# Two-tensor elementwise instructions on VectorE alone, in a list-scheduled encoder trunk of four layers

## The chip, the cores and the metric

The kernel runs on one core of a Trainium2 chip. The metric is the device time of one execution in microseconds (us); lower is better. Where several executions are given, the median is compared.

## What is computed

The reference is an encoder trunk of four residual layers over an input of 256 tokens by 1024 channels, in float32. Each layer is a token mixer followed by a SwiGLU feed-forward network (FFN), each behind an RMS norm and with its result added to the residual. The mixer is RWKV-7 time mixing in layers 0 and 3, stick-breaking attention in layer 1, and attention over keys selected by an indexer ("DSA") in layer 2.

```python
D_MODEL = 1024; SEQ = 256; DEPTH = 4; HEAD_DIM = 64; D_FF = 2816

def rms_norm(x, g):
    return x * lax.rsqrt(jnp.mean(x * x, axis=-1, keepdims=True) + RMS_EPS) * g

def swiglu(h, w_gu, w_down):
    g, u = jnp.split(h @ w_gu, 2, axis=-1)
    return (jax.nn.silu(g) * u) @ w_down

# end of rwkv7_time_mix: y is the output of the recurrence
    y = ((y - mu) * lax.rsqrt(var + RW_GN_EPS)).reshape(B, S, D) * ln_w + ln_b
    y = y + (jnp.sum(rh * kh * r_k, axis=-1, keepdims=True) * vh).reshape(B, S, D)
    out = (y * g).astype(h.dtype) @ w_out

# rope, used for the queries and keys of DSA
    return jnp.concatenate([x1 * cos - x2 * sin, x1 * sin + x2 * cos], axis=-1)
```

## The kernel before

**Tiles.** Channels lie on the partitions, tokens along the free dimension. The residual is four tiles `xt` of 128 partitions by 2 x 256 float32. Every weight is streamed from HBM in pieces of 128 x 1024 (`raw`) and split into a high part and the rest of it: `wh`, a cast (ScalarE or VectorE), and `wl = raw - wh`, always on VectorE. Activations are split in the same manner (`xg` for the normed input, `yhl`, `rhl`), and TensorE multiplies high by high, high by low and low by high.

**The order of the work.** Nothing is issued where it is written. Each call on a queue object (`pe`, `dve`, `act`, `pool`, `sp`, or `anye`, the "any" queue) is recorded by `Plan.record` (line 318), with a cost in ns from `_cost` (line 235). An instruction on `anye` is recorded with several engines as alternatives, from the table `ALTS` (line 201); one that reads or writes PSUM loses GpSimd as an alternative. `Plan._schedule` (line 420) then simulates the five engines with those costs: at each step the engine that is free first takes the ready instruction of the highest rank (the longest chain of costs behind it). An instruction with alternatives is skipped by an engine if another one would finish it earlier by the planner's costs (`elsewhere`, line 490); VectorE's cost counts double there (`BIAS = {"vector": 2.0}`). GpSimd's modelled cost of a two-tensor instruction is 2.1 ns per element of the row plus 150. `emit` (line 650) issues the planned list in its order; each engine works through its own part in that order, and the one line 661 issues every instruction of it. So L661 in the profile is not a place in the program, and the names of the tiles tell what an instruction is.

**Warm-up matmuls.** Where the planned TensorE has a gap, or where nothing ready keeps it filled enough, `keep_warm` (line 480) puts in two matmuls (`WARMERS = 2`) into a bank `warm_o` that nobody reads (line 1564).

**The instructions of `anye.tensor_tensor`.** There are five such lines:

```python
anye.tensor_tensor(nstate["acc"], nstate["acc"], sq, op=ALU.add)   # 836: sqa, before an FFN, stick or DSA
anye.tensor_tensor(nstate["acc"], nstate["acc"], sq, op=ALU.add)   # 848: sq, before an RWKV layer
anye.tensor_tensor(sd, sd, pr[:, p], op=ALU.add)                   # 1297: ysd, end of RWKV
anye.tensor_tensor(sd, sd, gT[:, p], op=ALU.mult)                  # 1298: ysd, end of RWKV
anye.tensor_tensor(b, a, cosb, op=ALU.mult)                        # 1435: rope in DSA (qk, sbt)
```

`prep_chunk` (line 826) prepares the input of the next sub-layer, one `xt` tile at a time as soon as the last output product has been added to it: a square on ScalarE (`sq`), its sum over the four tiles (`sqa`, on `anye`), and two `xg` pairs, the high half on ScalarE, the low one on VectorE. The FFN's first matmuls (`gate`, line 887 on) read `xg`; the sum `sqa` goes through TensorE into `rstd`, which is needed when the products are taken out of PSUM. In RWKV, `post` (line 1286) runs once for each of eight head pairs: variance by a matmul (`vb`), logarithm and exponential on ScalarE, a multiply, an affine step, the two `ysd` steps, and the split into `yhl`. Four `post` results make one half of the input of the output product `po` (`out_half`), which then is added to `xt`. In DSA `rope` splits its input (`rhl`) for an exact rotation on TensorE (`qrot` for queries and keys) and multiplies by the cosine on `anye`.

Of the kernel before, what the change touches and what calls it, by code (L numbers as in the profile page):

```python
# [187 lines left out]
class Queue:  # L188
# [5 lines left out]
    def __getattr__(self, method):  # L194
# [4 lines left out]
          AF.Tanh: "sigmoid_and_others", AF.Silu: "silu_and_others"}  # L199

ALTS = {("any", "copy"): [("scalar", "copy"), ("vector", "tensor_copy")],
        ("any", "tensor_tensor"): [("vector", "tensor_tensor"), ("gpsimd", "tensor_tensor")],
        ("any", "memset"): [("gpsimd", "memset"), ("vector", "memset")]}


# [1523 lines left out]
```

## Time and profile before

| | before |
|---|---|
| median of 3 executions | 1474.14 us (1473.09 to 1474.48) |
| the profiled execution | 1473.95 us |
| its span in the profile | 1472.2 us |
| mean granted TensorE clock | 0.999 |
| instructions in the span | 26233 |
| busy: TensorE (PE) | 1447.0 us, 10434 instructions |
| busy: VectorE (DVE) | 1107.1 us, 2026 |
| busy: ScalarE (ACT) | 718.3 us, 1348 |
| busy: GpSimd (POOL) | 61.3 us, 57 |

A row of the grouped instructions reads: line, engine, operation, written tile <- read tiles, shapes and types, count | busy us, mean ns of one | idle time of the engine just before them, and what ended most of it. A row of the timeline reads: start, duration, engine, line, operation, tiles, shape, count, and in brackets the engine's idle time before it with its releaser. A row of the waits reads: who waits <- for whom: total us, times, longest. PEld is TensorE's loading of weights, SP the engine that issues DMAs.

### The profile page before, as it was taken

The numbers are of one execution on the slowest core, as the hardware profiler recorded it, in microseconds if no ns is written. First come the engines' busy times: TensorE is split into PE (matmuls) and PEld (weight loads), VectorE is DVE, ScalarE is ACT, GpSimd is POOL, SyncE is SP. The second block draws the span as 40 slices with busy tenths as digits, with TensorE's granted clock in tenths as the row PEclk, the third lists the DMA queues.
The fourth block names the chain that finished last, engine by engine and source line by source line (L and its number), as shares of the span: only waits on it lengthen the run. The fifth ranks groups of instructions, "written<-read, shape, count | busy, mean of one in ns | idle before, by whom it ended". The sixth has DMA issues, their size and how long they took to land.

```text
span 1472.2 us, 26233 instructions
## 1 busy us (share of the span) xinstructions
PE 1447.0 (98%) x10434; PEld 1228.1 (83%) x10434; DVE 1107.1 (75%) x2026; ACT 718.3 (49%) x1348; POOL 61.3 (4%) x57
## 2 busy tenths in 40 slices
PE   9999999999999999999999989999999999999998
PEld 6788788888888888888977868888877877888887
DVE  7297478998566779986789978986474884789864
ACT  2344665444447655444546755444325256654442
POOL 0000010000000010000100010000100001200000
PEclk9999999999999999999999999999999999999999
DMA  7234135655554445555634445555523430455653
GB/s 254 91 107 144 36 101 172 194 183 194 175 183 136 130 158 186 198 187 181 192 113 130 129 144 172 186 193 183 197 93 108 129 101 18 130 175 182 196 188 132
DMA packets 77803, 224.55 MB, mean 153 GB/s; under 512 B 23536, under 2 KB 23792, under 8 KB 77424
## 3 DMA queue, kind: packets, MB, share of 16 engines
q1 hardware_dynamic: 77680, 222.87, 46.4%
q8 instruction: 82, 1.34, 0.4%
q14 instruction: 41, 0.34, 0.1%
HBM read 219.70 MB, written 3.15 MB: 151 GB/s over the span
## 4 chain that ended last, share of the span: by engine, by line
PE 86%; DVE 9%; ACT 2%; DMA 2%; issue 1%; SPq 0%; POOL 0%; DVEq 0%
PE up L661 17%; PE dn L661 16%; PE gate L661 16%; PE qk L661 5%; PE po L661 4%; PE kp L661 4%; PE rp L661 4%; PE vps L661 3%; PE z L661 2%; DVE wl L661 2%; PE vp L661 2%; PE warm_o L1564 1%; PE Y L661 1%; PE sc L661 1%; DVE xg L661 1%
## 5 line engine op out<-in xcount | busy, mean ns | idle before, releaser
L661 ACT CAST wh<-raw 128x1024 fp32r<-128x1024 f32 x317 | 329.7, 1050 | 401.8 <-PE dn L661 130.2
L661 DVE TENSOR_TENSOR wl<-raw,wh 128x1024 fp32r<-128x1024 f32 x349 | 420.3, 1222 | 70.0 <-ACT wh L661 58.5
L661 PE MATMUL gate<-xg,wh 128*128 128x512 f32 x704 | 259.9, 398 | 3.9 <-DVE xg L661 2.1
L661 PE MATMUL up<-xg,wh 128*128 128x512 f32 x704 | 259.9, 397 | 0.0
L661 PE MATMUL dn<-h,wh 128*128 128x512 f32 x704 | 247.6, 394 | 0.0
L661 PE MATMUL dn<-h,wl 128*128 128x256 f32 x704 | 197.5, 280 | 0.0
L661 PE MATMUL gate<-xg,wl 128*128 128x256 f32 x704 | 197.2, 280 | 0.0
L661 PE MATMUL up<-xg,wl 128*128 128x256 f32 x704 | 197.2, 280 | 0.0
L661 PEld LDWEIGHTS gate<-xg,wh 128*128 128x128 f32 x704 | 132.2, 188 | 38.1 <-DVE xg L661 3.4
L661 PEld LDWEIGHTS up<-xg,wh 128*128 128x128 f32 x704 | 132.2, 188 | 31.1
L661 PEld LDWEIGHTS dn<-h,wh 128*128 128x128 f32 x704 | 132.4, 188 | 30.8
L661 PEld LDWEIGHTS up<-xg,wl 128*128 128x128 f32 x704 | 132.8, 189 | 0.2
L661 PEld LDWEIGHTS gate<-xg,wl 128*128 128x128 f32 x704 | 132.8, 189 | 0.1
L661 PEld LDWEIGHTS dn<-h,wl 128*128 128x128 f32 x704 | 132.4, 188 | 0.0
L661 PE MATMUL qk<-xg,wh 128*128 128x256 f32 (+1 forms) x384 | 95.0, 326 | 0.1
L661 PE MATMUL qk<-xg,wl 128*128 128x256 f32 x256 | 72.0, 281 | 0.4 <-DVE wl L661 0.4
L661 PEld LDWEIGHTS qk<-xg,wh 128*128 128x128 f32 x384 | 64.2, 189 | 7.8 <-issue 1.4
L661 PE MATMUL kp<-pre,raw 128*128 128x256 f32 x256 | 59.9, 386 | 1.7 <-DVE pre L661 1.7
L661 DVE TENSOR_TENSOR gus<-gus,rstd 128x512 f32<-128x512 f32 x88 | 59.8, 687 | 1.2
L661 PE MATMUL vp<-xv,raw 128*128 128x256 f32 x256 | 59.0, 385 | 0.9 <-DVE vf L661 0.9
L661 PE MATMUL rp<-xr,raw 128*128 128x256 f32 x256 | 58.7, 382 | 0.0
L661 PEld LDWEIGHTS kp<-pre,raw 128*128 128x128 f32 x256 | 47.3, 190 | 13.3 <-issue 4.0
(292 smaller groups left out, 2355.5 us busy)
## 6 DMA issues: line engine op xcount, KB each, us to landing
raw<-in_wts_dram SPq DMA_DIRECT2D x397, 512.0 KB, 3.6
lora<-in_lora_dram SPq DMA_DIRECT2D x2, 1536.0 KB, 9.2
lg<-in_lora_dram SPq DMA_DIRECT2D x4, 512.0 KB, 5.4
xt<-in_xT_dram SPq DMA_DIRECT2D x4, 256.0 KB, 4.0
lora<-in_lora_dram SPq DMA_DIRECT2D x2, 512.0 KB, 5.6
xi<-in_id_dram SPq DMA_DIRECT2D x2, 512.0 KB, 8.0
scr<-SB SPq DMA_DIRECT2D x8, 128.0 KB, 3.4
xa<-scr SPq DMA_DIRECT2D x2, 512.0 KB, 3.3
```

The source lines that it names most:

```text
L661: getattr(getattr(nc, o.eng), method)(*map(real, args), **{k: real(a) for k, a in kw.items()})
L1564: lambda: [nc.tensor.matmul(wo[:, :S], wx[:, :P], wx, start=True, stop=True) for _ in range(WARMERS)])
```

## The change

```diff
--- before
+++ after
@@ -199,7 +199,7 @@
           AF.Tanh: "sigmoid_and_others", AF.Silu: "silu_and_others"}
 
 ALTS = {("any", "copy"): [("scalar", "copy"), ("vector", "tensor_copy")],
-        ("any", "tensor_tensor"): [("vector", "tensor_tensor"), ("gpsimd", "tensor_tensor")],
+        ("any", "tensor_tensor"): [("vector", "tensor_tensor")],
         ("any", "memset"): [("gpsimd", "memset"), ("vector", "memset")]}
```

The five lines above now have VectorE as their one choice. The table is read when an instruction is recorded, so the planner knows of it: it lays out the whole program anew. GpSimd keeps the memsets and the copies that are written for it.

In the program as built, the 40 two-tensor instructions that GpSimd had are on VectorE: 18 sums `sqa`, 10 `ysd` multiplies by `gT`, 6 `ysd` additions of `pr`, 4 rope multiplies, 2 sums `sq`. TensorE has the same matmuls apart from the warm-up ones, 332 where there were 294; 18 of the added ones are in the output product of each RWKV layer, the rest around DSA. In the FFNs the order of TensorE's instructions is the same. Some choices between ScalarE and VectorE (casts, copies, affine steps) fall differently.

## The prediction

> **What bounds the kernel now.** I read the page first: the busy table, then the chain that ended last.
>
> ```profile
> span 1472.2 us, 26233 instructions
> PE 1447.0 (98%) x10434; PEld 1228.1 (83%) x10434; DVE 1107.1 (75%) x2026; ACT 718.3 (49%) x1348; POOL 61.3 (4%) x57
> PE 86%; DVE 9%; ACT 2%; DMA 2%; issue 1%; SPq 0%; POOL 0%; DVEq 0%
> ```
>
> TensorE is busy for 1447.0 of 1472.2 us and makes 86% of the chain; VectorE makes 9%; GpSimd has none of it. Work saved elsewhere pays only where TensorE waits for it. The list of waits, restricted to TensorE, names those places (total, times, longest):
>
> ```profile
> PE qrot L661 <- DVE rhl L661: 2.7, 4, 1.7
> PE gate L661 <- DVE xg L661: 2.1, 4, 0.5
> PE vps L661 <- DVE wl L661: 1.5, 1, 1.5
> PE gate L661 <- DVE xt L661: 1.4, 4, 0.4
> PE pS L661 <- DVE Sn L661: 1.1, 2, 0.5
> PE po L661 <- DVE xt L661: 1.0, 2, 0.5
> PE po L661 <- ACT ysd L661: 0.8, 2, 0.4
> ```
>
> The two gate rows are the four starts of an FFN: 2.1 + 1.4 = 3.5 us. The pS and po rows are the ends of the two RWKV layers: 2.9 us. qrot and vps, 4.2 us, lie in the DSA layer. Nearly everywhere else TensorE is the limit itself, even where VectorE is dense: in this stretch of an FFN (columns: length, then busy time and count for PE, PEld, DVE, ACT, POOL) TensorE fills 114.11 of 115 us beside 102.11 us of VectorE.
>
> ```profile
> 525.00:640.00 115.00, 114.11 (x649) 99.14 (x648) 102.11 (x157) 55.97 (x76) 3.41 (x2) 1.00 0.55 182
> ```
>
> **What is removed and added.** By groups of instructions, shapes apart, GpSimd loses six:
>
> ```profile
> L661 POOL TENSOR_TENSOR sqa<-sqa,sq 128x512 f32<-128x512 f32 x18 | 28.7, 1595 | 555.3 <-ACT sq L661 490.8 <-issue 64.5
> L661 POOL TENSOR_TENSOR ysd<-ysd,gT 128x256 f32<-128x256 f32 x10 | 7.7, 772 | 212.0 <-DVE ysd L661 211.7
> L661 POOL TENSOR_TENSOR ysd<-ysd,pr 128x256 f32<-128x256 f32 x6 | 7.7, 1286 | 43.0 <-ACT ysd L661 43.0
> L661 POOL TENSOR_TENSOR qk<-qa,sbt 128x512 f32<-128x512 f32 x3 | 4.3, 1428 | 49.2 <-DVE qa L661 42.5 <-PE qk L661 6.7
> L661 POOL TENSOR_TENSOR sq<-sq 128x512 f32<-128x512 f32 x2 | 3.5, 1749 | 39.8 <-ACT sq L661 39.8
> L661 POOL TENSOR_TENSOR sbt<-sbt 128x512 f32<-128x512 f32 x1 | 2.3, 2274 | 10.2 <-DVE sbt L661 10.2
> ...
> L661 DVE TENSOR_TENSOR gus<-gus,rstd 128x512 f32<-128x512 f32 x88 | 59.8, 687 | 1.2
> L661 DVE TENSOR_TENSOR wl<-raw,wh 128x1024 fp32r<-128x1024 f32 x349 | 420.3, 1222 | 70.0 <-ACT wh L661 58.5 <-PE po L661 4.7 <-DMA scx<-xi 0.8
> L661 DVE SCALAR_TENSOR_TENSOR xg<-xt,vecs,xg 128x256 fp32r<-128x256 f32 x48 | 34.7, 759 | 0.0
> ```
>
> That is 40 instructions and 54.2 us. On VectorE a 128x512 one costs 0.687 us (the gus row), a 128x256 one 0.42 (a row below): 24 x 0.687 + 16 x 0.42 = 23.2 us added. But VectorE also loses a delay. The timeline at the first start of an FFN, VectorE and GpSimd:
>
> ```profile
> 215.96 2.71 DVE L661 SCALAR_TENSOR_TENSOR xg<-xt,vecs,xg 128x256 fp32r<-128x256 f32 x4
> 216.98 1.41 POOL L661 TENSOR_TENSOR sqa<-sqa,sq 128x512 f32<-128x512 f32 x1 [7.32 <-ACT sq L661]
> 218.59 0.67 DVE L661 TENSOR_TENSOR xt<-xt,po 128x512 f32<-128x512 f32 x1
> 220.92 0.47 DVE L661 SCALAR_TENSOR_TENSOR xg<-xt,vecs,xg 128x256 fp32r<-128x256 f32 x1
> 221.75 1.92 POOL L661 TENSOR_TENSOR sqa<-sqa,sq 128x512 f32<-128x512 f32 x1 [3.37 <-ACT sq L661]
> 222.45 2.29 DVE L661 SCALAR_TENSOR_TENSOR xg<-xt,vecs,xg 128x256 fp32r<-128x256 f32 x3
> ```
>
> One xg alone takes 0.47. Four with a step of about 0.40 would take 1.67, three 1.27; they take 2.71 and 2.29, 1.04 and 1.02 more, each time beside a GpSimd add. Over 48 xg the mean of 759 ns against 470 makes 48 x 0.289 = 13.9 us of such delay. So VectorE's load hardly grows; what counts is where.
>
> **Starts of an FFN, four times.** In the built order of the changed kernel TensorE's instructions are the same here. VectorE gets the first sqa add between xt (218.59) and the wl behind it, the other two behind the last xg. The chain xt, wl, xg, wl, xt, xg to the waiting gate matmul loses 1.04 + 1.02 and gains 0.69: 1.4 us shorter, and the bank that the first gate matmul waits for (xt) comes 1.04 earlier. Both exceed the waits of at most 0.4 and 0.5, so these go: -3.5 us. Behind the added instruction are queued that wl and three xg; their new slack of some 0.5 us is the cover, and without it an add would cost up to 0.69 each, 2.7 in all. The third add feeds rstd, needed only when gate and up of the first block are evicted; VectorE does it sooner than GpSimd's 1.5.
>
> **Ends of RWKV, twice.** The changed order puts 18 warm-up matmuls (warm_o) into the output product, where there were none. Rows of before:
>
> ```profile
> 200.38 0.42 DVE L661 TENSOR_TENSOR ysd<-ysd,gT 128x256 f32<-128x256 f32 x1
> 203.65 0.60 PE L661 MATMUL vb<-ysq,consts 128*128 128x256 f32 x2
> 209.86 1.21 DVE L661 TENSOR_TENSOR wl<-raw,wh 128x1024 fp32r<-128x1024 f32 x1
> 211.00 0.42 DVE L661 TENSOR_TENSOR yhl<-ysd,yhl 128x256 fp32r<-128x256 f32 x1
> 217.83 0.40 PE L661 MATMUL po<-yhl,wh 128*128 128x256 f32 x2
> 218.54 0.39 PE L661 MATMUL po<-yhl,wh 128*128 128x256 f32 x2
> 218.77 0.28 PE L661 MATMUL po<-yhl,wl 128*128 128x256 f32 x1
> 861.42 2.56 PE L1564 MATMUL warm_o<-warm_x 128*128 128x256 bf16 x22
> ...
> L1564 PE MATMUL warm_o<-warm_x 128*128 128x256 bf16 x294 | 44.0, 285 | 1.2 <-DVE eps_rms L661 1.2
> ```
>
> From the last vb to the last po there are 18 units of work (one unit is 218.54 - 217.83 = 0.71 us) and it takes 219.05 - 203.65 = 15.4 us. In the new order: vb 0.45, 3 units 2.1, 18 warmers at 2.56 / 22 = 0.116 each 2.1, then 15 units, the first of which needs the second yhl. On VectorE that yhl stands behind wl, xt, a copy, two multiplies, two affines, an add, a wl and a multiply. An instruction starts about 0.08 before the one ahead has ended (209.86 + 1.21 against 211.00), so the steps are 2 x 1.14 + 0.61 + 7 x 0.34 + 0.42 = 5.7 us from a wl that starts some 0.4 before the last vb: ready at 5.3, where TensorE stands at 4.65. It waits 0.6, then 0.3 in two pieces for later banks and yhl, and drains 0.3: 0.45 + 12.8 + 2.1 + 0.9 + 0.3 = 16.5, or +1.1 a layer. Here nothing hides the warmers but the wait they fill: without them it would be 2.7 us long. Bounds: -1.4 a layer (the waits of before go, as the ysd steps no longer take GpSimd's 1.3) and +2.1 (all warmers are extra). I take +1.1, near the row-by-row count: +2.2 for both.
>
> **DSA.** Four multiplies move into a stretch where VectorE is nearly always busy.
>
> ```profile
> 762.71 1.68 DVE L661 CAST wh<-raw 128x1024 fp32r<-128x1024 f32 x1
> 778.07 0.69 DVE L661 CAST wh<-raw 128x1024 fp32r<-128x1024 f32 x1
> 795.28 1.96 DVE L661 TENSOR_TENSOR wl<-raw,wh 128x1024 fp32r<-128x1024 f32 x1
> 808.22 1.62 DVE L661 TENSOR_TENSOR rhl<-qa,rhl 128x512 fp32r<-128x512 f32 x1
> ```
>
> Beside GpSimd's multiplies the cast lost 0.99, wl 0.74, rhl 0.93: 2.7 us, against 3 x 0.687 = 2.1 added in the same place. Each qrot wait shrinks by about 0.3, less two extra warmers: -0.6. The last pairs are only reordered; I take 0, with bounds of -1 and +2.
>
> **Elsewhere** (sqa at the other starts of layers, sq before the second RWKV): VectorE has idle time and TensorE does not wait; 0, or 0.7 for one that met a wait.
>
> The sum: -3.5 + 2.2 - 0.6 = -1.9. The profiled execution took 1473.95 us, span 1472.2 and 1.75 around it, 0.2 under the median of 1474.14. 1473.95 - 1.9 = 1472.0 us. About 0.2% (3 us) is what a measurement of this kernel can tell from no change; the forecast lies inside it.
>
> **A rule against the change.** The Trainium skill, Perfetto Trace Analysis, section Optimizing Scalar/DVE Operations, says that where VectorE is saturated it may make sense to hand work to ScalarE or even GpSimd, and adds that between VectorE and GpSimd, which share a read port, it might not help. The first half is the first rival; the second agrees with the stretched xg, 0.47 against some 1.5.
>
> **Rivals.** *VectorE becomes the bound in RWKV's tail and in DSA* (slower). All 16 ysd steps (6.7) and 4 multiplies (2.8) fall on the path, 9.5, and only the 3.5 is won back: +6.0, 1480.0. For: behind the last vb VectorE has hardly a gap. Against: TensorE has work from the first half of the product beside the earlier eight, and the delays end too. It decides from the point where the wait for the second yhl exceeds the 0.6 by 2.5 a layer; with half on the path it is 1477. Chance 0.18. By the rule's first half alone the sum would be this one.
>
> *GpSimd's long steps were the wait* (faster). Then both tails lose their waits, -2.9, DSA -1.0, the FFN starts -3.5: 1473.95 - 7.4 = 1466.6. For: ysd<-ysd,pr takes 1.29 there and 0.42 here. Against: the warmers fill 2.1 us in any case. Chance 0.25.
>
> *The planner undoes it*: choices elsewhere move so that nothing remains; the built order has no two-tensor instruction on GpSimd, so only by chance. 1473.95, chance 0.02.
>
> **Numbers.** The forecast has 0.55, its own range 1469 to 1475.5 by the bounds above. A quarter of it lies below 1471.0, a small part above 1476.9. Faster 0.25 + 0.13 = 0.38, slower 0.17 + 0.02 = 0.19, same 0.43. Range 1467.0 to 1477.0: it leaves out half of either rival.
>
> **What would show it.** The gate waits for xg and xt gone from TensorE's list; xg at a mean near 480 ns; no TENSOR_TENSOR on POOL; 332 warm_o in place of 294; about 16.5 us from the last vb to the last po; a first qrot wait near 0.8. Wrong would be: gate waits still there, a wait of over 2 us for yhl behind the warmers, or new waits in DSA's last pairs.

## The result, and the profile after

| | before | after |
|---|---|---|
| median of 6 executions each | 1474.31 us (1473.09 to 1475.66) | 1464.51 us (1463.87 to 1467.24) |
| ratio, 95% interval | 1 | 0.9937 (0.9924 to 0.9950) |
| profiled execution, span | 1473.95, 1472.2 us | 1466.17, 1464.4 us |

The change takes 9.8 us off the median; by the interval it is 7.4 to 11.2. The forecast was 1472.0, its range 1467 to 1477: the direction was right, the size was not, and the time lies below the range. The same three lines of the page, of after:

```profile
span 1464.4 us, 26299 instructions
...
PE 1444.4 (99%) x10472; PEld 1229.7 (84%) x10472; DVE 1104.8 (75%) x2067; ACT 712.3 (49%) x1347; POOL 8.0 (1%) x17
...
PE 90%; DVE 7%; DMA 1%; ACT 1%; issue 1%; SPq 0%; DVEq 0%; POOL 0%; POOLq 0%
```

VectorE has 41 instructions more and is busy 2.3 us less: 23 us of work were added and about as much went, more than half of it delay of xg (34.7 to 21.2 us). TensorE executes 38 more matmuls and is busy 2.6 us less, which cannot be work; this row is taken up below. The waits of TensorE, of after:

```profile
PE pT L661 <- DVE prs L661: 1.7, 2, 1.0
PE gate L661 <- DVE xt L661: 1.6, 4, 0.4
...
PE vps L661 <- DVE wl L661: 1.4, 1, 1.4
PE po L661 <- DVE yhl L661: 1.4, 4, 0.6
...
PE qrot L661 <- DVE rhl L661: 0.8, 1, 0.8
...
PE po L661 <- DVE xt L661: 0.3, 2, 0.2
```

The gate wait for xg is gone; a gate wait for xt is still listed, but at another matmul (below). qrot fell from 2.7 to 0.8. And the groups that the forecast named:

```profile
L1564 PE MATMUL warm_o<-warm_x 128*128 128x256 bf16 x332 | 48.7, 282 | 1.2 <-DVE eps_rms L661 1.2
...
L661 DVE SCALAR_TENSOR_TENSOR xg<-xt,vecs,xg 128x256 fp32r<-128x256 f32 x48 | 21.2, 477 | 0.0
...
L661 DVE TENSOR_TENSOR sqa<-sqa,sq 128x512 f32<-128x512 f32 x18 | 12.3, 683 | 0.0
L661 DVE TENSOR_TENSOR rhl<-qa,rhl 128x512 fp32r<-128x512 f32 x8 | 5.5, 687 | 0.2 <-ACT rhl L661 0.2
```

xg takes 477 ns where it took 759, and a sum that GpSimd made in 1.6 us takes VectorE 0.68.

**Where the time went.** TensorE's matmuls are the same in both kernels apart from warm-up ones, so the program can be cut at the same matmuls in every trace and the pieces compared. An FFN start reaches from the end of the last po before it to the end of its four ss matmuls (in layer 0: 219.04 to 243.50 before, 220.43 to 243.71 after); a tail of RWKV from the start of its first vb to the end of its last po; DSA's first part from the first qrot to the first po, its second part from there to the last qrot. The stick-breaking layer, the rest of each FFN and DSA's two ends agree within 0.1 us between before and after.

| us against before | four FFN starts | DSA, first part | DSA, second part | two tails | sum |
|---|---|---|---|---|---|
| forecast | -3.5 | -0.6 | 0 | +2.2 | -1.9 |
| after | -4.83 | -1.75 | -1.68 | +0.15 | -8.1 |

The rest of the program, its first 14 us and the two RWKV bodies, came out 0.3 longer in this execution, and differs between executions with the same order: the eleven below stand between -1.4 and +2.4 there, apart from one with a lowered clock. An example is the fourth square of the kernel's first norm, which waits for its input from HBM; before, then after, ScalarE in the timeline:

```profile
7.48 0.63 ACT L661 ACTIVATE sq<-xt 128x512 f32<-128x512 f32 x1 [1.12 <-DMA xt<-in_xT_dram]
```

```profile
8.65 0.63 ACT L661 ACTIVATE sq<-xt 128x512 f32<-128x512 f32 x1 [2.02 <-DMA xt<-in_xT_dram]
```

This 1.08 us is not of the change: a second execution of the changed kernel (below) started as before did, within 0.05. So the stages account for 8.1 of the measured 9.8 us, inside its interval.

### The profile page after: what moved, and what is told of

The parts are those of the page before. It is cut to its first block, busy times and chain, and to the rows that moved or that the text cites. A ratio compares the mean times of both kernels' runs of the same rounds, so it can differ in the third digit from the quotient of the medians.

```text
span 1464.4 us, 26299 instructions
## 1 busy us (share of the span) xinstructions
PE 1444.4 (99%) x10472; PEld 1229.7 (84%) x10472; DVE 1104.8 (75%) x2067; ACT 712.3 (49%) x1347; POOL 8.0 (1%) x17
## 4 chain that ended last, share of the span: by engine, by line
PE 90%; DVE 7%; DMA 1%; ACT 1%; issue 1%; SPq 0%; DVEq 0%; POOL 0%; POOLq 0%
PE up L661 17%; PE gate L661 17%; PE dn L661 17%; PE qk L661 5%; PE po L661 5%; PE kp L661 4%; PE rp L661 4%; PE vps L661 3%; PE vp L661 2%; PE z L661 2%; PE warm_o L1564 1%; PE sc L661 1%; PE Y L661 1%; DVE wl L661 1%; PE attn_o L661 1%
## 5 line engine op out<-in xcount | busy, mean ns | idle before, releaser
L661 ACT CAST wh<-raw 128x1024 fp32r<-128x1024 f32 x313 | 325.6, 1050 | 403.0 <-PE dn L661 130.4
```

The lines of the kernel that those rows point to most:

```text
L661: getattr(getattr(nc, o.eng), method)(*map(real, args), **{k: real(a) for k, a in kw.items()})
```

## The experiments

All ratios are to the kernel before on the same chip, whose median there was 1475.6 (first four), 1475.9 (next four) and 1475.9 us (last three). The stage columns are those of the table above, each from one profiled execution.

| kernel | median, us | ratio (95%) | FFN starts | DSA 1 | DSA 2 | tails |
|---|---|---|---|---|---|---|
| e1: order of before, VectorE | 1472.22 | 0.9979 (0.9964 to 0.9993) | -3.43 | -1.00 | -0.01 | +1.55 |
| e2: order of after, GpSimd | 1471.26 | 0.9971 (0.9957 to 0.9986) | -0.25 | -1.10 | -1.68 | +0.75 |
| e3: sqa back | 1470.22 | 0.9965 (0.9951 to 0.9979) | -0.30 | -1.78 | -1.67 | +0.13 |
| e4: shadow additions | 1470.37 | 0.9967 (0.9953 to 0.9981) | -1.01 | -0.23 | -1.66 | +0.14 |
| e5: after again | 1464.94 | 0.9938 (0.9917 to 0.9959) | -4.73 | -1.73 | -1.63 | +0.12 |
| e6: no tail warm-ups | 1467.02 | 0.9938 (0.9916 to 0.9959) | -4.84 | -1.76 | -1.63 | +1.65 |
| e7: rope back | 1469.19 | 0.9954 (0.9935 to 0.9974) | -4.80 | +0.01 | +0.01 | +0.15 |
| e8: ysd back | 1466.73 | 0.9939 (0.9917 to 0.9961) | -4.80 | -1.73 | -1.63 | +0.14 |
| e9: late sums | 1464.45 | 0.9920 (0.9897 to 0.9943) | -5.70 | -1.79 | -1.63 | +0.17 |
| e10: shadow memsets | 1465.55 | 0.9925 (0.9903 to 0.9948) | -4.72 | -1.71 | -1.62 | +0.13 |
| e11: shadow copies | 1466.48 | 0.9928 (0.9898 to 0.9957) | -3.94 | -1.41 | -1.62 | +0.06 |

A stage that an experiment does not touch repeats within 0.15 us, which is far finer than the medians.

**Engine or order (e1, e2).** The change does two things: it puts 40 instructions on another engine, and it makes the planner lay out a new order. e1 keeps the old order and swaps the engine on issue:

```diff
             if not o.instrs:
                 nc.scalar.preload_act_table_set(o.table)
+            eng = o.eng
+            if eng == "gpsimd" and [m for m, _, _ in o.instrs] == ["tensor_tensor"]:
+                eng = "vector"
             for method, args, kw in o.instrs:
-                getattr(getattr(nc, o.eng), method)(...)
+                getattr(getattr(nc, eng), method)(...)
```

> The order planned for the kernel before is kept, and the 40 instructions planned for GpSimd are issued on VectorE at the same places of the order. Theory G (what went is GpSimd's own time and the delay it puts on VectorE; the new order matters little): about 1465 us, the four FFN starts some 1.2 shorter each, DSA some 3 shorter, as in the changed kernel. Theory P (the gain is the new order, warm-up matmuls included): within 2 us of before, 1472 to 1476. If G holds and the 18 added warm-up matmuls of each RWKV tail cost their full 2.1 us, this kernel, which lacks them, comes out near 1460 to 1461.

e2 is after's order with the same 40 on GpSimd, `eng = "gpsimd" if o.idx in MOVED else o.eng`, where MOVED lists them.

> The other corner: the order of the changed kernel is kept, and the same 40 instructions are issued on GpSimd. Theory G: the gain is gone, 1474 us or some us above it (VectorE's order was not planned around GpSimd's longer steps), mean of xg back near 760 ns, gate waits for xg back. Theory P: within 2 us of the changed kernel, 1463 to 1467.

Neither theory holds alone. e1 gained 0.2%: its 1472.22 lies among P's numbers, but 3.4 us under before on its own chip, more than the 2 us that P allows. e2 gained 0.3% and lies between the two. The stages say why: the FFN starts follow the engine (-3.43 with it alone; with GpSimd in the new order only -0.25 is left), DSA's second part follows the order (-0.01 in the old one, -1.68 in the new one, whatever the engine), DSA's first part takes about 1.0 of either, and the tails get worse by either alone (+1.55, +0.75) and come out even when both go together. The groups and waits of e2 show the old delay in the new order:

```profile
L667 DVE SCALAR_TENSOR_TENSOR xg<-xt,vecs,xg 128x256 fp32r<-128x256 f32 x48 | 34.7, 758 | 0.0
```

```profile
PE gate L667 <- DVE xg L667: 2.1, 4, 0.5
...
PE qrot L667 <- DVE rhl L667: 1.7, 1, 1.7
```

**The FFN starts (e3).** The table `ALTS` gets a queue "either" with both engines, and line 836 uses it:

```diff
+        ("either", "tensor_tensor"): [("vector", "tensor_tensor"), ("gpsimd", "tensor_tensor")],
...
-                anye.tensor_tensor(nstate["acc"], nstate["acc"], sq, op=ALU.add)
+                either.tensor_tensor(nstate["acc"], nstate["acc"], sq, op=ALU.add)
```

> The changed kernel with GpSimd given back as a choice for line 836 alone (the 18 sums sqa). TensorE's order is that of the changed kernel. Theory G: the four FFN starts give back the some 1.2 us each that they lost, 1464.5 + 4.8 = 1469.3 us; tails, DSA's middle and the second RWKV layer stay as in the changed kernel. Theory P: 1464.5 us within 1.

Theory G holds: all four starts gave back what they had lost, 4.5 of 4.83, and no other stage of the table moved. The 18 sums alone bring the long xg back (13 of the 48, as in before), and the wait with them; groups and waits of e3:

```profile
L662 DVE SCALAR_TENSOR_TENSOR xg<-xt,vecs,xg 128x256 fp32r<-128x256 f32 x48 | 34.7, 758 | 0.0
```

```profile
PE gate L662 <- DVE xg L662: 2.1, 4, 0.5
...
PE gate L662 <- DVE xt L662: 1.1, 4, 0.3
```

**Contention, or waiting for GpSimd's result (e4, e10, e11).** In the changed kernel, 24 of the moved instructions also set off work on GpSimd that nobody reads:

```diff
+    def shadow(src):
+        nc.gpsimd.tensor_copy(trig, src[:, 0, 0:1])
+        nc.gpsimd.tensor_tensor(scr, scr, scr, op=ALU.add)
```

> The changed kernel, in which each of the 18 sqa, 2 sq and 4 rope instructions also sets off an addition of a 128x512 scratch tile on GpSimd that nobody reads (behind a one-column copy of the same input). VectorE keeps all its work. Contention (an instruction of VectorE is stretched while GpSimd works on SBUF): mean of xg back from 477 ns towards 700, gate waits for xg back, 1468 to 1473 us. Latency (the gain came from no longer waiting for GpSimd's results): 1464.5 us within 1, xg near 480 ns.

In e10 the second line is `for _ in range(3): nc.gpsimd.memset(scr, 0.0)`, in e11 `for _ in range(2): nc.gpsimd.tensor_copy(scr[:, :S], scr[:, S:])`.

> The shadow kernel again, with three memsets of the 128x512 scratch tile in place of each addition (some 1.4 us of GpSimd writing and reading nothing; the one-column copy ahead is kept). It is also the control for that copy. If only GpSimd's reading of two tensors stretches VectorE: mean of xg stays near 480 ns and the time is that of the changed kernel within 1.5 us. If any work of GpSimd on SBUF does: xg 600 ns or more, 1468 to 1472 us.

> The shadow kernel with two copies of 128x256 in place of each addition (GpSimd reads one tensor and writes one). If one tensor read is harmless: xg near 480 ns, the changed kernel's time within 1.5 us. If a copy stretches VectorE as an addition does: xg 600 ns or more and 1468 to 1472 us.

The groups of the three, e4, e10 and e11 in this order:

```profile
L1574 POOL TENSOR_TENSOR shade<-shade 128x512 f32<-128x512 f32 x24 | 33.1, 1379 | 0.0
L667 DVE SCALAR_TENSOR_TENSOR xg<-xt,vecs,xg 128x256 fp32r<-128x256 f32 x48 | 27.5, 608 | 0.0
```

```profile
L1575 POOL MEMSET shade<- 128x512 f32 x72 | 38.3, 532 | 2.8
L667 DVE SCALAR_TENSOR_TENSOR xg<-xt,vecs,xg 128x256 fp32r<-128x256 f32 x48 | 21.3, 479 | 0.0
```

```profile
L1575 POOL COPY shade<-shade 128x256 f32<-128x256 f32 x48 | 33.4, 695 | 1.5
L667 DVE SCALAR_TENSOR_TENSOR xg<-xt,vecs,xg 128x256 fp32r<-128x256 f32 x48 | 23.2, 518 | 0.0
```

GpSimd works about as long in each, 33 to 38 us; what differs most is what it reads, beside the number and length of its instructions. Memsets leave xg at 479 ns and the FFN starts at -4.72; copies stretch it to 518 and give back 0.8 of 4.7; two-tensor additions stretch it to 608 and give back 3.7, and in DSA 1.5 of 1.75. e4 and e10 came out as contention by reading would have it; e11 lies between its two cases. Contention is shown; the memset kernel, which keeps the one-column copy, shows that the copy is not it. One reservation: in e4 1.8 us of TensorE's gate wait are put down to ScalarE's sq, whose one buffer the copy may still hold while it queues behind the additions, so not all of the 3.7 need be stretched xg. This wait stands at the matmul that waits for xt in after; with the 0.4 for xt that e4 still has, 2.2 us stand where after has 1.6:

```profile
PE gate L667 <- ACT sq L667: 1.8, 3, 0.7
```

The timeline of e4, VectorE and GpSimd at the first FFN start, shows that it goes both ways:

```profile
221.13 1.21 DVE L667 TENSOR_TENSOR wl<-raw,wh 128x1024 fp32r<-128x1024 f32 x1
221.21 2.03 POOL L1574 TENSOR_TENSOR shade<-shade 128x512 f32<-128x512 f32 x1
222.26 2.05 DVE L667 SCALAR_TENSOR_TENSOR xg<-xt,vecs,xg 128x256 fp32r<-128x256 f32 x3
...
225.84 1.04 POOL L1574 TENSOR_TENSOR shade<-shade 128x512 f32<-128x512 f32 x1
...
226.28 1.69 DVE L667 TENSOR_TENSOR wl<-raw,wh 128x1024 fp32r<-128x1024 f32 x1
```

The wl that began first keeps its 1.21, and GpSimd's addition takes 2.03 instead of 1.04; then xg, which began while the addition ran, is the one that is late. At 226.28 the addition is ahead, keeps its 1.04, and wl takes 1.69.

The means hide that an xg is either held up or not. In before 13 of the 48 xg took 1.50 to 1.53 us and the others 0.47 or 0.48; in e4 8 took 1.25 to 1.27, in e11 14 took 0.61 or 0.62. One of each with the GpSimd instruction beside it, before, e4 and e11:

```profile
216.98 1.41 POOL L661 TENSOR_TENSOR sqa<-sqa,sq 128x512 f32<-128x512 f32 x1 [7.32 <-ACT sq L661]
217.14 1.52 DVE L661 SCALAR_TENSOR_TENSOR xg<-xt,vecs,xg 128x256 fp32r<-128x256 f32 x1
```

```profile
216.38 1.21 POOL L1574 TENSOR_TENSOR shade<-shade 128x512 f32<-128x512 f32 x1
216.61 1.27 DVE L667 SCALAR_TENSOR_TENSOR xg<-xt,vecs,xg 128x256 fp32r<-128x256 f32 x1
```

```profile
217.07 0.67 POOL L1575 COPY shade<-shade 128x256 f32<-128x256 f32 x1
217.40 0.62 DVE L667 SCALAR_TENSOR_TENSOR xg<-xt,vecs,xg 128x256 fp32r<-128x256 f32 x1
```

In all 35 of these cases xg ends 0.27 to 0.29 us after the GpSimd instruction. So the delay follows how long that instruction lasts, and the copies cost little because each is short: 0.40 us where nothing holds it up, against 1.04 for an addition. That reading two tensors is worse than reading one is not shown. The Trainium skill, SBUF — State Buffer, section Who interferes with whom, has this as a rule: an exclusive lock on a port pair that VectorE and GpSimd share, taken by a VectorE instruction with two SBUF inputs against a GpSimd one that reads SBUF, not one that only writes, and the later one waits. The three kernels agree: 608 and 518 ns against readers, 479 against a writer.

**DSA (e7).** Line 1435 on the queue "either".

> The changed kernel with GpSimd given back as a choice for line 1435 alone (rope; three or four instructions go back). TensorE's order differs from the changed kernel's only inside DSA, where it is that of before. If the rope multiplies and the order that they bring are the whole of DSA's 3.4 us: DSA as long as before, 1464.5 + 3.4 = 1468 us, with every other stage as in the changed kernel. If DSA's gain came from elsewhere (sums sqa, choices of engine): 1465 us within 1.

Both parts of DSA return to before, +0.01 each, and no other stage of the table moves. (DSA's end, outside the table, is 0.3 longer, as also in e3 and e9, which leave rope alone.) So the rope multiplies are all of DSA's 3.4 us, directly and through the order that the planner builds once they are short. The waits of e7:

```profile
PE qrot L662 <- DVE rhl L662: 2.7, 4, 1.7
```

**The tails (e6, e8), with after as the base (e5).**

> The changed kernel unaltered, as the base for the three others on the same chip: ratio to before 0.9937 as measured first, about 1464.5 us.

e6 leaves out 36 warm-up matmuls by their planned time:

```diff
             if o.warmer:
-                warmer()
+                if not any(lo < o.start < hi for lo, hi in ((205e3, 207e3), (1256.5e3, 1258.5e3))):
+                    warmer()
                 continue
```

> The changed kernel without the 18 warm-up matmuls in the output product of each RWKV layer (36 in all; nothing else is touched). Cover (the prediction's step: they fill a wait for the second yhl that would be there without them): the changed kernel within 1 us, and the wait of po for yhl grows by about 2 us in each tail. Cost (they hold TensorE up): each tail is up to 2.1 us shorter, 1460 to 1462 us.

The second theory falls, as no tail became shorter, and the step of the first is there: TensorE's wait for yhl grows from 1.4 (after) to 5.4, by 2.0 a tail:

```profile
PE po L662 <- DVE yhl L662: 5.4, 4, 2.5
```

In the first tail nothing else changed. In the second one the granted clock was lower after the wait of 2.5 us, and that tail came out 1.5 longer. Stretches of e6 there, then of e5 at the same place (length, PE, PEld, DVE, ACT, POOL busy, granted clock, DMA share, GB/s):

```profile
1262.00:1268.00 6.00, 3.31 (x18) 2.97 (x17) 5.71 (x12) 1.12 (x3) 0.00 (x0) 0.81 0.49 162
1268.00:1274.00 6.00, 6.00 (x48) 6.00 (x48) 3.38 (x4) 3.78 (x7) 0.00 (x0) 0.91 0.35 98
```

```profile
1257.00:1263.00 6.00, 5.30 (x44) 4.69 (x44) 6.00 (x15) 2.59 (x6) 0.00 (x0) 1.00 0.52 155
1263.00:1269.00 6.00, 6.00 (x53) 6.00 (x52) 4.61 (x6) 3.82 (x7) 0.00 (x0) 1.00 0.41 128
```

So the warm-up matmuls cost nothing, and they may save. By the median e6 is not "within 1 us" but 2.1 above e5: five of its six executions took 1466.2 to 1469.7 us at a mean granted clock of 0.997 or 0.998, where ten of e5's twelve took 1464.0 to 1465.9 at 0.999 or 1.000. The ratios, each uncertain by 0.002, do not tell the two apart. e8 puts lines 1297 and 1298 on "either"; TensorE's order in the tails is then that of before.

> The changed kernel with GpSimd given back as a choice for lines 1297 and 1298 (the ysd steps). TensorE's order in the RWKV tails is that of before, without the 18 warm-up matmuls. If the ysd part of the change is worth nothing on the net, as the stages of the first two traces say: 1464.5 us within 1.5. If it costs +1.1 a layer, as predicted: 1462.3. If it gains (GpSimd's long steps were the wait): 1467 or more.

Ratio 0.9939 against 0.9938 and tails +0.14 against +0.12: in these stages the ysd part of the change is worth nothing on the net. The median, 1466.73, is 1.8 above e5's, just outside the 1.5 that was allowed for this case; e8 lacks the 36 warm-up matmuls too, so a gain of about that size outside the table is not excluded. (The profiled execution of e8 had a granted clock of 0.66 between 140 and 180 us, in the first RWKV body, outside the stages of the table.)

**A version with the sums later (e9).** The sums before an FFN wait for the xg pairs of the next tile, with two buffers for sq:

```diff
-                anye.tensor_tensor(nstate["acc"], nstate["acc"], sq, op=ALU.add)
+                nstate.setdefault("late", []).append(sq)
...
+            last = plan.ops[-1]
+            while len(nstate.get("late", [])) > (j < 3):
+                anye.tensor_tensor(nstate["acc"], nstate["acc"], nstate["late"].pop(0), op=ALU.add)
+                plan.after(plan.ops[-1], [last])
```

> The changed kernel with each sqa sum before an FFN put behind the xg pairs of the next tile (two buffers for sq instead of one); TensorE's order is the changed kernel's. The prediction said that an added sum between xt and the wl behind it has slack for cover. If the 0.4 us wait of gate that is left at each FFN start is that sum (0.68 us on VectorE): each start 0.4 to 0.7 us shorter, 1464.9 - 2 = 1463 us. If the wait is that of the transfer chain po, xt, xg itself: 1464.9 us within 0.5.

The wait for xt shrinks from 1.6 to 0.6, and each start by about 0.25:

```profile
PE gate L661 <- DVE xt L661: 0.6, 3, 0.2
```

By the stages this is 0.9 to 1.0 us better than after, half of what was hoped; the medians, 1464.45 against 1464.51 and 1464.94 measured at other times, cannot tell the two apart.

## Why the prediction was wrong

By the stages the forecast missed 6.2 us: 2.8 in DSA, 2.05 in the tails, 1.3 at the FFN starts.

**What held.** VectorE's load did not grow (forecast: hardly grows; busy 1107.1 to 1104.8). xg came to 477 ns (forecast near 480), warm_o to 332, GpSimd lost its two-tensor instructions, the first qrot wait fell to 0.8 (forecast 0.8). The mechanism at the FFN starts was the forecast one, delay beside GpSimd's sums, and e3 and e4 show it.

**FFN starts: right mechanism, mis-sized, -4.83 for -3.5.** The step was "both exceed the waits of at most 0.4 and 0.5, so these go: -3.5", a sum over the list of waits. Both waits did go, at each of the four starts. But the cover that the step counted on for the added sum ("their new slack of some 0.5 us") did not hold: behind it the next xt came later, and the ninth gate matmul, which had waited 0.1 before, waited 0.4 for it. This is the row for xt in the list of after, and e9, with the sum moved away, halves it. The first wait for xt of before and the new one of after, TensorE in the timeline:

```profile
219.41 0.47 PE L661 MATMUL gate<-xg,wh 128*128 128x512 f32 x1 [0.36 <-DVE xt L661]
```

```profile
222.23 0.47 PE L661 MATMUL gate<-xg,wh 128*128 128x512 f32 x1 [0.39 <-DVE xt L661]
```

So the list lost only 1.9, and most of the 4.83 came from matmuls that had waited while they were recorded as busy, a term that the step did not have. The gate matmuls at the first start, before and then after, 33 in each:

```profile
L661 PE MATMUL gate<-xg,wh 128*128 128x512 f32 x33 | 12.5, 406 | 1.0 <-DVE xg L661 0.5 <-DVE xt L661 0.4
```

```profile
L661 PE MATMUL gate<-xg,wh 128*128 128x512 f32 x33 | 12.2, 397 | 0.4 <-DVE xt L661 0.4
```

The idle time falls by 0.6, and the same 33 matmuls are recorded 0.3 shorter. Counting for each only its time beyond the end of the one before, they take 8.5 and 7.9, so half of the 1.2 of this start stood in TensorE's busy time. This, with the same in DSA, is why TensorE's busy time on the page fell while it did more.

**Tails: right inside its window, and the window was too short.** From the last vb to the last po the forecast had 15.4 become 16.5. Timeline of after, TensorE:

```profile
203.62 0.81 PE L661 MATMUL vb<-ysq,consts 128*128 128x256 f32 x3
...
206.41 2.14 PE L1564 MATMUL warm_o<-warm_x 128*128 128x256 bf16 x18
208.30 0.36 PE L661 MATMUL po<-yhl,wh 128*128 128x256 f32 x1
209.22 0.39 PE L661 MATMUL po<-yhl,wh 128*128 128x256 f32 x1 [0.55 <-DVE yhl L661]
```

The wait for the second yhl was 0.55 (forecast 0.6), the warm-up matmuls 2.1 (2.1), without them it was 2.5 (2.7), and the stretch grew by 1.20 (1.1). But the same new order had made the stretch from the first to the last vb 1.14 shorter (TensorE's waits of pS for Sn, 1.1 in the two layers, are gone there), and the forecast counted only from the last vb on. The term was +2.2 for two layers; it is +0.15.

**DSA: -3.43 for -0.6, the largest miss.** The step took each qrot wait as 0.3 shorter, "less two extra warmers", and for the last pairs "only reordered; I take 0, with bounds of -1 and +2". The -0.6 did not fit its own sign: a first qrot wait of 0.8 where it had been 1.7 is 0.9 already, and 0.3 from each of the three others makes 1.8. That is what the list lost (2.7 to 0.8, the three later waits altogether), and the first part came out at -1.75, its idle time 4.4 before and 2.6 after. There were not two but eight extra warm-up matmuls in it, 0.9, and other matmuls counted 0.9 less. e1 and e2 show that engine and order bring about 1.0 each when either is there alone. The reordered part is -1.68, outside its bounds, and belongs to the order alone. Of it, idle time is 0.3; qrot, pT and qss, counted beyond the end of the matmul before, are 0.9 shorter, and six warm-up matmuls are fewer there, 0.5. So zero was not a neutral value for a reordering: the planner, freed of a 1.3 us step, found a better order.

**The rivals.** "GpSimd's long steps were the wait" gave 1466.6, the nearest number, but by other stages: it had the two tails lose 2.9 together, which they did not, and DSA 1.0. VectorE did not become the bound. No case in the list had a large gain in DSA, and 1467 as lower end came from that list.

**What stays open.** The stages explain 8.1 us, the medians say 9.8, and the interval holds both. A wait of vp for vf in the second RWKV body (0.9 in the trace of before) also stood in e1 and in e6, whose order there is that of after, so it is not counted as gained. But it is absent from the other ten traces with that order, so about 1.0 us of the rest may belong to the change; no run isolates it. The granted clock moves this body too: in e1, e4, e6 and e9 it was 0.50 there for 3.4 us, and 28 vp matmuls took 8.00 us in e9 that took 6.31 in after.

## What to carry to other kernels

An instruction sent to GpSimd was paid for twice here when it read SBUF beside a busy VectorE: once by its own time and once by the VectorE instruction that is held up, 13.5 us of delay on xg alone for 54 us of GpSimd work; look for groups whose mean exceeds the fastest of the same shape, look at their single instructions, and line them up with GpSimd's timeline. The list of waits can understate what TensorE loses, since a matmul that waits is partly recorded as busy (3.5 us listed at the FFN starts, 1.6 of it left, 4.83 gained): cut both traces at the same matmuls and compare the pieces instead. Where a planner lays the program out anew, compare whole stages, and keep an unexplained reordering's bounds wide on both sides.

## What the runs showed of the hardware

VectorE's xg was held up by GpSimd instructions that read SBUF and not by memsets, which only write: of 48 xg, 13 took 1.5 us beside the sums, 8 took 1.26 beside the shadow additions, 14 took 0.62 beside the shadow copies, against 0.47 alone; beside memsets the mean stayed at 479 ns. Each of these held-up xg ended 0.27 to 0.29 us after the GpSimd instruction.

After a TensorE wait of 2.5 us the granted clock was 0.81 and then 0.91 in one tail of e6 (means over 6 us) and 1.00 in the other, so the wait alone does not decide. A wait is not needed either. Stretches of e9 in the second RWKV body, where TensorE was busy throughout:

```profile
1160.00:1168.00 8.00, 8.00 (x47) 6.42 (x46) 3.83 (x14) 2.64 (x8) 0.00 (x0) 1.00 0.73 222
1168.00:1171.40 3.40, 3.40 (x9) 2.73 (x9) 3.30 (x13) 3.31 (x9) 0.00 (x0) 0.51 0.40 163
```

The Trainium skill, TensorE: Matmul & The Clock Gate, section HAM oscillation — how this bites in real kernels, puts the danger at idle gaps above about 3.4 us. The gap in e6 was shorter, and e9 has none there; what lowered the clock stays open.
